# RoPE on one core: the last software load cut into 16 and 48 rows instead of 32 and 32, and GpSimd's first store tied to the 16

## The chip, the cores and the metric

The kernel runs on one core of one Trainium2 chip. The metric is device microseconds (us) of that core for one execution. Before the change the median of 11 runs is 85.08 us, from 84.03 to 87.63. The profile that is read below is of one execution that took 85.83 us, of which 84.1 us are the profiled span.

## The reference

```python
def setup_inputs():
    batch, n_heads, seq, head_dim = 8, 8, 1024, 64
...
    angles = np.outer(positions, freqs)
    cos = np.cos(angles)
    sin = np.sin(angles)
    x_first, x_second = x[:, :, :, :half], x[:, :, :, half:]
    out_first = x_first * cos - x_second * sin
    out_second = x_first * sin + x_second * cos
    return np.concatenate([out_first, out_second], axis=-1).astype(np.float32)
```

`x` has 8 x 8 = 64 heads of 1024 rows of 64 float32 values. One head is 256 KB, all of `x` is 16.8 MB, and so is the output. `positions` has 1024 whole numbers and `freqs` 32 floats.

## The kernel before, in words

**Tiling.** A head is cut into 16 chunks of 64 rows (`C = 64`), and one chunk lies in one partition, as a run of 64 x 64 = 4096 values (`run`). Eight heads fill 128 partitions (`G = 8`). `groups` (line 43) lists eight groups: the first has six heads (96 partitions), the other seven have eight heads. The two heads left over (`edge = 2`, heads 0 and 1) take another way: SP loads them in float32 (line 69) and stores them at the very end (line 175).

**Loads.** GpSimd issues all loads of the groups at the start (lines 77 to 83). They convert float32 in HBM to bf16 in SBUF on the way, so that a partition's run is 16 KB when it is read and 8 KB when it lands. Each group is one DMA, apart from the last group, which comes as two: the first 32 rows of every chunk and then the other 32. That makes nine DMAs. The DMA semaphores are used in turn, eight of them, so the ninth load waits until the first has landed (10.37 us).

**Tables.** VectorE (DVE) and ScalarE (ACT) make the sine and cosine tables of the chunked layout (`tables`, line 92). A second, smaller pair of tables, for the two edge heads, is made after the third group (lines 153 to 156). The instruction that rounds the turns is line 99.

**Rotation.** For each group DVE does three operations (`rotate`, line 134): a product with the sine (line 138), a product with the cosine (139) and a sum with the two halves swapped (141).

**Stores.** GpSimd issues one store for each group (line 151), which converts bf16 to float32 on the way out. All loads and all stores of the groups go through GpSimd's one software DMA queue, q0. Ahead of the first store stands line 145, an instruction that does nothing but wait until the first part of the last group's load has landed:

```python
    nc.gpsimd.keepalive_nop(ins=[nc.gpsimd.lower_ap(xts[-1][:, :run // 2])])
```

Behind it, each store waits in order for the sum of its group. By then several groups are ready.

**End.** SP waits for the landing of all group stores but the last (lines 172 and 173), issues two stores of 256 KB for the edge heads (line 175), and waits for the end of everything (lines 176 to 178).

Of the kernel before, what the change touches and what calls it, by code (L numbers as in the profile page):

```python
# [10 lines left out]
def kernel(  # L11
# [7 lines left out]
    nc = tc.nc  # L19
# [6 lines left out]
    b, h, seq, d = x.shape  # L26
# [14 lines left out]
    run = C * d  # L41
    first = G - edge
    groups = [(edge, first)] + [(g, G) for g in range(G, bh, G)]
# [7 lines left out]
    def hbm(t, lo, n, a=0, b=run):  # L51
        return bass.AP(tensor=t.tensor, offset=t.offset + lo * head + a,
                       ap=[[run, n * chunks], [1, b - a]])
# [14 lines left out]
    for i in range(edge):  # L68
        nc.sync.dma_start(out=xf[:, i], in_=hbm_head(x, i))
    nc.scalar.dma_start(  # L70
        out=pos_i[:chunks].bitcast(positions.dtype),
        in_=bass.AP(tensor=positions.tensor, offset=positions.offset, ap=[[C, chunks], [1, C]]))
    nc.scalar.dma_start(out=fr[0:P:32], in_=freqs[None, :].to_broadcast([P // 32, half]))


    xts = []
    for lo, n in groups:
        xt = xpool.tile([P, run], bf16, name="xt")[:n * chunks]
        parts = 2 if lo == groups[-1][0] else 1
        for a in range(0, run, run // parts):  # L80
            b = a + run // parts
            nc.gpsimd.dma_start(out=xt[:, a:b], in_=hbm(x, lo, n, a, b))  # L82
        xts.append(xt)
    half_pi = singles.tile([P, 1], f32)
    nc.gpsimd.memset(half_pi, math.pi / 2)
# [28 lines left out]
    for q in range(0, P, 32):  # L114
        v.tensor_copy(out=pos_f[q:q + 32],  # L115
                      in_=pos_i.rearrange("p (c w) -> p c w", w=words)[:, :, :1])
# [5 lines left out]
        out=pos_r.bitcast(positions.dtype),  # L122
        in_=bass.AP(tensor=positions.tensor, offset=positions.offset,
                    ap=[[R, P], [1, R], [1, 1]])))
# [17 lines left out]
        return ot  # L142


    nc.gpsimd.keepalive_nop(ins=[nc.gpsimd.lower_ap(xts[-1][:, :run // 2])])

    stored = []
    for i, ((lo, n), xt) in enumerate(zip(groups, xts)):
# [60 lines left out]
```

## Time and profile before

| what | us |
|---|---|
| median of 11 runs | 85.08 (84.03 to 87.63) |
| the profiled execution | 85.83 |
| its span | 84.1 |
| DVE busy | 65.1 |
| ACT busy | 9.4 |
| POOL (GpSimd) busy | 10.1 |
| ninth load issued | 10.37 |
| first store issued | 42.35 |
| last group store issued | 71.39 |
| SP's two stores issued | 77.12 |

The span is the time from the first to the last recorded instruction of the execution; what lies around it is 85.83 - 84.1 = 1.73 us. The page cuts the span into 40 slices of 2.1 us; a digit is the busy share of a slice in tenths. Its GB/s count the bytes on the destination's side, so that a load that lands as bf16 shows half of what it reads. HBM read is 16.79 MB and written 16.78 MB, 399 GB/s over the span.

### The profile page before, as it was taken

To read this page: it belongs to the slowest core of one execution; us is meant where nothing else is said; L and a number is where in the kernel's file an instruction comes from. 1 tells how busy PE (TensorE), PEld (TensorE's weight loads), DVE (VectorE), ACT (ScalarE), POOL (GpSimd) and SP (SyncE) were. 2 spreads that over 40 slices of the span, in tenths; PEclk is the share of its full clock that TensorE was granted. 3 is DMA by queue.
4 is the path that set the end of the run, shared out by engine and by line. 5 is a ranking of instruction groups with operands and counts; after the bars stand their busy time and mean duration, and the time that the engine had idled before them with its cause. 6 is when DMAs were issued, how large, how long until landed. Compare 5 with 4: busy or idle time off the path is not lost.

```text
span 84.1 us, 155 instructions
## 1 busy us (share of the span) xinstructions
DVE 65.1 (77%) x46; ACT 9.4 (11%) x8; POOL 10.1 (12%) x22
## 2 busy tenths in 40 slices
DVE  0125995499999999999999999999999999900000
ACT  0600004997000000000006000000000000000000
POOL 4960050000000000000081000200200200200000
DMA  2999999999999999999969999999999999999992
GB/s 16 296 211 187 203 210 222 210 226 207 220 208 218 214 214 218 210 211 209 185 222 413 413 452 398 468 405 452 421 444 429 437 429 405 460 413 444 405 389 110
DMA packets 3144, 25.45 MB, mean 303 GB/s; under 512 B 504, under 2 KB 520, under 8 KB 1288
## 3 DMA queue, kind: packets, MB, share of 16 engines
q0 software_dynamic: 2384, 24.38, 94.9%
q1 hardware_dynamic: 576, 1.05, 3.7%
q10 hardware_dynamic: 184, 0.02, 0.3%
HBM read 16.79 MB, written 16.78 MB: 399 GB/s over the span
## 4 chain that ended last, share of the span: by engine, by line
DVE 65%; issue 12%; DMA 7%; ACT 2%; ACTq 1%
DVE ot L139 21%; DVE ot L141 16%; DVE t L138 14%; DMA const<-in_freqs_dram 7%; DVE turnsc L95 3%; DVE turnsc L101 3%; ACT sinc L105 2%; DVE wholec L99 1%; DVE last L166 1%; DVE last L163 1%; DVE sinc L106 1%; DVE t L163 1%; ACTq L70 1%; DVE turnsr L95 0%; DVE turnsr L101 0%
## 5 line engine op out<-in xcount | busy, mean ns | idle before, releaser
L138 DVE TENSOR_TENSOR t<-xt,sinc 128x4096 bf16<-128x4096 bf16 (+1 forms) x8 | 18.2, 2281 | 0.0
L139 DVE TENSOR_TENSOR ot<-xt,cosc 128x4096 bf16<-128x4096 bf16 (+1 forms) x8 | 18.2, 2281 | 0.0
L141 DVE TENSOR_TENSOR ot<-ot,t 128x4096 bf16<-128x4096 bf16 (+1 forms) x8 | 18.2, 2280 | 0.0
L151 POOL DMA_DIRECT2D out_dram<-ot x8 | 4.2, 533 | 56.0 <-DMA xt<-in_x_dram 30.7
L82 POOL DMA_DIRECT2D xt<-in_x_dram x9 | 5.6, 640 | 5.6 <-DMA xt<-in_x_dram 4.7
L105 ACT ACTIVATE sinr<-turnsr 128x256 bf16<-128x256 f32 x1 | 0.4, 417 | 23.4 <-DVE turnsr L101 23.4
L105 ACT ACTIVATE sinc<-turnsc 128x2048 bf16<-128x2048 f32 x1 | 1.9, 1909 | 9.9 <-DVE turnsc L101 9.9
L101 DVE TENSOR_TENSOR turnsc<-turnsc,wholec 128x2048 f32<-128x2048 f32 x1 | 2.3, 2293 | 0.0
L95 DVE TENSOR_TENSOR turnsc<-pos_f,fturn 128x2048 f32<-128x2048 f32 x1 | 2.3, 2293 | 0.0
L106 DVE TENSOR_SCALAR sinc<-sinc 128x2048 bf16<-128x2048 bf16 x1 | 0.7, 694 | 2.0 <-ACT sinc L105 2.0
L87 DVE LOAD_MASK_SELECT const<-const x1 | 0.0, 14 | 2.8 <-DMA const<-in_positions_dram 2.8
L109 ACT ACTIVATE cosc<-wholec,half_pi 128x2048 bf16<-128x2048 f32 x1 | 2.0, 2002 | 0.1
L108 ACT ACTIVATE wholec<-turnsc 128x2048 f32<-128x2048 f32 x1 | 1.9, 1894 | 0.0
L88 DVE LOAD_MASK_SELECT const<-const x1 | 0.0, 14 | 2.4 <-DMA const<-in_freqs_dram 2.4
L105 ACT ACT_TABLE_LOAD x1 | 1.3, 1283 | 2.6 <-issue 2.6
L99 DVE TENSOR_SCALAR wholec<-turnsc 128x2048 f32<-128x2048 f32 x1 | 1.2, 1226 | 0.0
L166 DVE TENSOR_TENSOR last<-last,t 128x1024 f32<-128x1024 f32 x1 | 1.2, 1225 | 0.0
L163 DVE TENSOR_TENSOR last<-x,cosr 128x1024 f32<-128x1024 bf16 x1 | 1.2, 1214 | 0.0
L126 ACT CAST x<-xf 128x1024 bf16<-128x1024 f32 x1 | 1.0, 1028 | 0.0
L115 DVE CAST pos_f<-const 32x64 f32<-32x64 int32 x4 | 0.8, 194 | 0.1
L64 DVE MEMSET const<- 128x160 int32 x1 | 0.2, 192 | 0.8 <-PEq L193 0.8
L109 ACT ACTIVATE cosr<-wholer,half_pi 128x512 bf16<-128x512 f32 x1 | 0.7, 722 | 0.0
(15 smaller groups left out, 3.7 us busy)
## 6 DMA issues: line engine op xcount, KB each, us to landing
out_dram<-ot POOLq DMA_DIRECT2D x7, 2048.0 KB, 12.4
xt<-in_x_dram POOLq DMA_DIRECT2D x6, 1024.0 KB, 23.8
out_dram<-ot POOLq DMA_DIRECT2D x1, 1536.0 KB, 5.5
xt<-in_x_dram POOLq DMA_DIRECT2D x2, 512.0 KB, 35.2
xt<-in_x_dram POOLq DMA_DIRECT2D x1, 768.0 KB, 8.8
xf<-in_x_dram SPq DMA_DIRECT2D x2, 256.0 KB, 2.9
out_dram<-last SPq DMA_DIRECT2D x2, 256.0 KB, 5.5
const<-in_positions_dram ACTq DMA_DIRECT2D x1, 8.0 KB, 2.7
```

What stands on the lines that cost most here:

```text
L82: nc.gpsimd.dma_start(out=xt[:, a:b], in_=hbm(x, lo, n, a, b))
L95: v.tensor_mul(out=turns, in0=pos_f.to_broadcast([P, n, half]), in1=fturn.to_broadcast([P, n, half]))
L99: v.tensor_scalar(out=whole, in0=turns, scalar1=magic, scalar2=magic, op0=Alu.add, op1=Alu.subtract)
L101: v.tensor_sub(out=turns, in0=turns, in1=whole)
L105: nc.scalar.activation(out=sin[:, :, 0], in_=turns, func=Act.Sin, scale=twopi)
L109: nc.scalar.activation(out=cos, in_=whole[:, :, None, :].to_broadcast([P, n, copies, half]), func=Act.Sin, scale=-twopi, bias=half_pi)
L138: v.tensor_mul(out=t.rearrange(flat), in0=xt, in1=sin_c[:n].rearrange(flat))
L139: v.tensor_mul(out=ot, in0=xt.rearrange("p (c two h) -> p c two h", two=2, h=half), in1=cos_c[:n].to_broadcast([n, C, 2, half]))
L141: v.tensor_add(out=ot, in0=ot, in1=swap(t))
L151: nc.gpsimd.dma_start(out=hbm(out, lo, n), in_=ot.rearrange("p c two h -> p (c two h)")))
L163: v.tensor_mul(out=o, in0=x0, in1=w.rearrange("p r two h -> p (r two h)")[:, None, :].to_broadcast(flat))
L166: v.tensor_add(out=last.rearrange(rows, two=2, h=half), in0=last.rearrange(rows, two=2, h=half), in1=swap(t.rearrange(rows, two=2, h=half)))
```

## The change

The last group's two loads are cut at 16 rows instead of 32. The first part has 1024 values a partition (4 KB read, 2 KB landed), the second 3072 (12 KB read, 6 KB landed). The number of DMAs and their order are as before. Line 145 waits for the first part, which is now the 16 rows.

```diff
+    first_part = run // 4
     xts = []
     for lo, n in groups:
         xt = xpool.tile([P, run], bf16, name="xt")[:n * chunks]
-        parts = 2 if lo == groups[-1][0] else 1
-        for a in range(0, run, run // parts):
-            b = a + run // parts
-            nc.gpsimd.dma_start(out=xt[:, a:b], in_=hbm(x, lo, n, a, b))
+        cut = first_part if lo == groups[-1][0] else run
+        for a, b in ((0, cut), (cut, run)):
+            if a < b:
+                nc.gpsimd.dma_start(out=xt[:, a:b], in_=hbm(x, lo, n, a, b))
         xts.append(xt)
...
-    nc.gpsimd.keepalive_nop(ins=[nc.gpsimd.lower_ap(xts[-1][:, :run // 2])])
+    nc.gpsimd.keepalive_nop(ins=[nc.gpsimd.lower_ap(xts[-1][:, :first_part])])
```

## The prediction

> **What bounds the kernel now.** I read the page's slices first.
>
> ```profile
> DVE  0125995499999999999999999999999999900000
> DMA  2999999999999999999969999999999999999992
> ```
>
> DVE ends five slices before the end; DMA is at 9 in every slice from the second to the last but one, with one dip, slice 21 (42.0 to 44.1 us). So the kernel is a string of transfers: all loads, then all stores. The chain of waits follows DVE, which is no contradiction: it doesn't see that a store stands in the DMA queue behind others. The trace's semaphore events confirm the string. A full group load lands every 4.87 us (last engine at 14.84, 19.71, 24.60, 29.48, 34.34, 39.21), a full store likewise (47.88, 52.75, ... 81.92). Both move 2 MB on the HBM side: 2.097 MB / 4.87 us = 431 GB/s.
>
> Next the dip, in the stretches view (columns: us, busy time of DVE, ACT and POOL, clock, DMA share, GB/s):
>
> ```profile
> 40.00:41.00 1.00, 1.00 (x1) 0.00 (x0) 0.00 (x0) 1.00 1.05 213
> 41.00:42.00 1.00, 1.00 (x3) 0.00 (x0) 0.00 (x0) 1.00 0.83 164
> 42.00:43.00 1.00, 1.00 (x1) 0.00 (x0) 0.65 (x2) 1.00 0.19 37
> 43.00:44.00 1.00, 1.00 (x3) 0.04 (x1) 1.00 (x3) 1.00 0.73 283
> ```
>
> Against the 1.05 of full work the three stretches lose 0.22 + 0.86 + 0.32 = 1.40 us, as a mean over 16 DMA engines. The waits and the timeline name the wait in front of the first store:
>
> ```profile
> POOL out_dram L151 <- DMA xt<-in_x_dram: 30.7, 1, 30.7
> ```
> ```profile
> 41.11 0.28 DVE L99 TENSOR_SCALAR wholer<-turnsr 128x256 f32<-128x256 f32 x1
> 41.31 2.28 DVE L141 TENSOR_TENSOR ot<-ot,t 128x4096 bf16<-128x4096 bf16 x1
> 42.35 2.11 POOL L151 DMA_DIRECT2D out_dram<-ot  x4 [30.67 <-DMA xt<-in_x_dram]
> ```
>
> The share 0.19 is the clue: 0.19 x 16 = 3 engines work on while 13 stand idle. The trace's single DMA packets and landings say the same. Each DMA raises its semaphore 16 times, once an engine. The first 32 rows landed on 13 engines at 39.48 to 39.95, on the other three at 41.23, 41.53, 41.67. Three engines are 1.7 us behind; they were so from the first load (7.73 to 8.00 against 9.59 to 10.09), where packets of 1.5 to 2.0 us stand in place of 0.63. The 13 ended their loads at 41.6 to 42.1, the three at 43.46, 43.64, 43.77. The first store packets start at 43.44 on the idle engines, and at 43.6 to 43.8 on the last ones. **So the three late engines never waited**: their store packets were queued (43.44) before their own loads ended. The dip belongs to the 13 that are ahead.
>
> **What the Trainium skill says.** "DMA: Bandwidth & Descriptors", section "Why a DMA increments its semaphore by 16 and not by 1": with a software DMA all 16 engines post their +1, and only the full count says that it has landed. So the slowest engine opens line 145, as the landings here show. Same page, "Where 436 GB/s comes from": 16 ports of 32 B at 850 MHz, 435 GB/s; the 431 measured is at that, in loads and stores. A lane at its own ceiling can't be helped by others: while 13 engines were idle, the three late ones' packets took 322 to 324 ns, as when all worked. "SBUF — State Buffer", section "SBUF: two separate sides": a DVE operation in a two-port mode keeps GpSimd from writing its DMA descriptors, until its end + about 115 ns. The trace agrees: the ninth load's issue took 1.20 us instead of the 0.54 to 0.65 of the others, beside line 99's float32 operation (10.22 to 11.45), and ended at 11.57.
>
> **The change part by part.** I work in the profiled span.
>
> 1. *First part.* Half a load took 41.67 - 39.21 = 2.46 us for 8 packets an engine: 307 ns each for 4 KB landed; 8 KB takes 4.87 / 8 = 609. The slope is 302 ns for 4 KB, the fixed part 5 ns. A 2 KB packet is then 5 + 151 = 156 ns (estimate), eight are 1.25 us, and the slowest engine lands at 39.21 + 1.25 = 40.46, 1.21 us earlier.
> 2. *Second part.* A 6 KB packet is 5 + 453 = 458 ns (estimate), eight are 3.66. Both parts: 4.91 us against 4.92 before. No packet is added (8 + 8 an engine), no DMA either. So the loads end when they ended: 41.6 to 42.1, and 43.77 on the last engine. The nearest rows don't show a 6 KB packet; from packet lengths instead (324 and 625 ns) the fixed part is 2 x 324 - 625 = 23 ns. At one extra packet a row that is 8 x 23 = 0.18 us; from below it can't gain, the bytes being the same. I take 0.
> 3. *The issues.* The ninth load is issued at 10.37 as before, since it waits for the first load, not for its size; its 1.20 us hide behind 30 us of queued loads. No load is queued later.
> 4. *The wait at line 145.* From landing to issue it took 42.35 - 41.67 = 0.68, from issue to the first store packet 43.44 - 42.35 = 1.09. Now: issue at 41.14, packets at 42.23. Line 99's small operation (41.11 to 41.39) may hold the issue until 41.39 + 0.12 and a further 0.5 at most: packets at 42.23 to 42.6. It covers itself: nobody but the 13 idle engines waits.
> 5. *Behind it on GpSimd*: the stores of groups 1 to 4. Groups 1 to 3 have been ready since 38.65, so they are issued at 41.1, 41.7, 42.2. Group 4's sum ends at 43.59, so its issue moves only from 43.93 to about 43.7. Three stores are 22 heads, 5.8 MB, at 431 GB/s some 13 us of work, so no engine runs dry; later stores are issued at 53.2, 59.8, 66.4, 71.4 by DVE, at least 5.6 us ahead of the landing of the store before (the seventh lands at 77.05).
> 6. *The 13 engines* start stores at about 42.3 instead of 43.5: 1.2 us ahead. **The three late ones start at 43.5 to 43.8, as before.** From there each has 62 store packets of 608 ns: 43.77 + 37.7 = 81.5; the last group's packets ended at 81.54. Nothing moves.
> 7. *SP* issues its two stores after the seventh store's last landing (77.05, issue at 77.12), which a late engine sets. Their packets follow the last group's on each engine (81.1 to 82.8). Unmoved.
>
> Sum on the path: 0 + 0 + 0, less at most 0.1 us where an engine now ahead had been last at the end. Span 84.1 to 84.0; that execution took 85.83, and would take 85.8. Against the median of the runs, 85.08 - 0.05, I say 85.0.
>
> If in another execution no engine is late, the first half lands at about 39.95, store packets are there at 39.95 + 1.77 = 41.72, and the loads end at 41.6 to 42.1. There is no dip to close either, or one of 0.1 us.
>
> **Rivals.**
>
> *A, the dip is the gain.* If the work left were shared among all engines, the signal's 1.21 us would come off: 85.08 - 1.21 = 83.9. For it: the dip is real, 1.40 us. Against it: every store puts 8 packets on each engine (the first one 6), whichever is free, and the three late engines stay 1.7 us behind through all seven loads without catching up. Chance 0.08.
>
> *B, reads and writes collide (slower).* 13 engines would write for 1.5 us while three read. Where stores began at 44.1, single packets took 951, 904 and 780 ns instead of 642, up to 48% more. Were the late engines' last 1.5 us stretched so, it is +0.7; doubled, and lasting, +1.5: 85.8 to 86.6. It passes 1% from a stretch of 57% (0.85 / 1.5). Against it: the late engines' last load packets, between 43.44 and 43.77, ran beside writes and took 324 ns at most. Chance 0.09.
>
> *C, the 6 KB rows are cut small (slower).* At 23 ns a packet and 8 rows an engine, 1% (0.85 us) takes 5 more packets a row; 512 B pieces (12 a row) cost 8 x 11 x 23 ns = 2.0: 87.1. Rows of 8 KB and 16 KB stay whole in the trace. Chance 0.05.
>
> **How the numbers follow.** My case (nothing moves, within 0.3 us either way) has 0.78. About 1% is what a measurement of this kernel can tell from no change. Faster by over 1%: A, 0.08, and 0.01 from the tail of my case. Slower: B and C, 0.14. Within 1%: 0.77. The range goes down to A (84.0) and up to the whole of B (86.6), leaving out C; the likeliest case alone is 84.7 to 85.3.
>
> **What would show it.** Right: the first part lands on the last engine near 40.5 and the first store is issued near 41.1; the dip in the slices is gone or small; first store landings spread over about 1.5 us (the engines ahead near 46.4, the late ones near 47.8) instead of 0.41; SP's stores at about 77.1. Wrong: SP's issue a full us earlier (A); load packets over 324 ns after 42.3 (B); more than 16 load packets of the last group an engine (C); or an execution in which even the last engine had stood idle before.

## The result, and the profile after

The changed kernel takes 85.67 us (median of 12 runs, 84.80 to 87.02), the kernel before, run beside it, 85.53 us (47 runs, 83.80 to 87.63). The ratio is 1.0098, 95% interval 1.0057 to 1.0139: slower by about 0.8 us. The two medians hide most of that, because in many executions of these kernels a few DMA engines fall 1 to 2 us behind at the start, and the ratio leaves out the executions with the longest times. The shortest spans agree with it: 82.0 to 82.1 us many times in the timed executions of the kernel before, 82.7 in the shortest of the changed kernel's twelve.

The profiled execution of the changed kernel took 84.81 us, with a span of 82.7. That is less than the 84.1 of the profile before, though the kernel is slower: no engine fell behind in it (first load landed at 7.52 to 7.91 on all 16), whereas three had in the other. Two single profiles of this kernel can't be compared by their spans.

The slices of the changed kernel (same rows as before, with GB/s added):

```profile
DVE  0147993699999999999999999999999999930000
DMA  1999999999999999999999999999999999999992
GB/s 16 309 222 218 206 226 202 226 218 202 228 208 214 226 202 230 206 193 167 223 399 412 452 412 444 444 412 444 412 444 444 412 452 404 444 444 412 460 344 76
```

The dip in DMA is gone, but this profile doesn't show that the change closed it: no engine is late here, and for such an execution the prediction expected no dip, or one of 0.1 us, in the kernel before either. The GB/s row has a dip where the DMA row shows none: it falls to 193 and 167 in slices 18 and 19 (35 to 39 us), from some 214. The engines are busy there, but they move less. The wait and the first stores:

```profile
POOL out_dram L152 <- DMA xt<-in_x_dram: 30.9, 1, 30.9
```
```profile
39.73 1.59 POOL L152 DMA_DIRECT2D out_dram<-ot  x3 [30.89 <-DMA xt<-in_x_dram]
40.54 0.36 DVE L100 TENSOR_SCALAR wholer<-turnsr 128x256 f32<-128x256 f32 x1
43.38 0.53 POOL L152 DMA_DIRECT2D out_dram<-ot  x1 [2.07 <-DVE ot L142]
```

The first three stores go out together and the fourth waits for DVE, as forecast. The stretches of the changed kernel (us, DVE, ACT, POOL, clock, DMA share, GB/s):

```profile
36.00:37.00 1.00, 1.00 (x1) 0.00 (x0) 0.00 (x0) 1.00 0.84 162
37.00:38.00 1.00, 1.00 (x2) 0.00 (x0) 0.00 (x0) 1.00 1.07 143
38.00:39.00 1.00, 1.00 (x3) 0.00 (x0) 0.00 (x0) 1.00 1.18 209
39.00:40.00 1.00, 1.00 (x1) 0.00 (x0) 0.27 (x1) 1.00 1.04 215
40.00:41.00 1.00, 1.00 (x3) 0.00 (x0) 1.00 (x3) 1.00 0.98 203
41.00:42.00 1.00, 1.00 (x1) 0.00 (x0) 0.31 (x1) 1.00 1.09 266
42.00:43.00 1.00, 1.00 (x1) 0.00 (x0) 0.00 (x0) 1.00 1.05 416
43.00:44.00 1.00, 1.00 (x3) 0.54 (x2) 0.53 (x1) 1.00 1.16 475
```

and of the kernel before where its 32-row part begins:

```profile
36.00:37.00 1.00, 1.00 (x2) 0.00 (x0) 0.00 (x0) 1.00 0.80 164
37.00:38.00 1.00, 1.00 (x1) 0.00 (x0) 0.00 (x0) 1.00 1.11 225
38.00:39.00 1.00, 1.00 (x3) 0.00 (x0) 0.00 (x0) 1.00 1.05 213
```

From 37 to 38 us the engines are as busy as ever (1.07 against 1.11) and move 143 instead of 225 GB/s. (The 36-to-37 line is alike in both: a packet counts where it starts.) The single packets of the trace say why. There are 128 packets of 2 KB for the 16 rows. The 48 that start before 37.03 us take 172 or 173 ns each; of the 80 that start later, 56 take longer, up to 414 ns, and the mean of the 80 is 258. The 6 KB packets take 474, apart from seven that start between 38.13 and 38.78 us and take 484 to 600.

**A measure that leaves out what happens at the start.** I count from the landing of the seventh group's load on its last engine to the last landing of SP's stores. So the 1 to 2 us that an engine lost in the first load drop out. The parts are differences of the trace's landing events, each on its last engine, in us:

| profiled execution | 7th load lands | first part | whole 8th load | from 7th load to the end |
|---|---|---|---|---|
| before | 39.21 | 2.46 | 4.93 | 43.96 |
| before, again | 39.02 | 2.46 | 4.93 | 44.01 |
| before, third | 39.76 | 2.46 | 5.00 | 43.95 |
| changed kernel | 37.16 | 1.89 | 5.70 | 44.63 |

The eighth load takes 5.70 - 4.93 = 0.77 us longer, and 1.89 - 1.25 = 0.64 of it lies in the first part, measured against the forecast. The end comes 44.63 - 43.96 = 0.67 us later, counted from the same point. The ratio says 0.8 us, with an interval of about 0.5 to 1.2, so 0.67 agrees with it.

### The profile page after: what moved, and what is told of

It reads as the page before. It is cut to its first block, busy times and chain, and to the rows that moved or that the text cites. A ratio compares the mean times of both kernels' runs of the same rounds, so it can differ in the third digit from the quotient of the medians.

```text
span 82.7 us, 155 instructions
## 1 busy us (share of the span) xinstructions
DVE 65.5 (79%) x46; ACT 9.4 (11%) x8; POOL 9.5 (11%) x22
## 4 chain that ended last, share of the span: by engine, by line
DVE 66%; issue 12%; DMA 6%; ACT 2%; ACTq 1%
DVE ot L140 21%; DVE ot L142 16%; DVE t L139 14%; DMA const<-in_freqs_dram 6%; DVE turnsc L102 3%; DVE turnsc L96 3%; ACT sinc L106 2%; DVE wholec L100 1%; DVE last L167 1%; DVE last L164 1%; DVE sinc L107 1%; DVE t L164 1%; ACTq L70 1%; DVE turnsr L96 0%; DVE turnsr L102 0%
## 5 line engine op out<-in xcount | busy, mean ns | idle before, releaser
L83 POOL DMA_DIRECT2D xt<-in_x_dram x9 | 4.9, 566 | 3.4 <-DMA xt<-in_x_dram 2.6
```

## The experiments

Two theories run through the expectations. The first says that the 16 rows cost, being short rows that leave gaps in HBM. It is called S at first and R later; G and L are two forms of it. The rival, called C at first and W later, says that the early store costs, because stores are queued behind loads that still run.

**The early wait on the loads of before.** Stores as early as can be, no short rows:

```diff
-    nc.gpsimd.keepalive_nop(ins=[nc.gpsimd.lower_ap(xts[-1][:, :run // 2])])
+    nc.gpsimd.keepalive_nop(ins=[nc.gpsimd.lower_ap(xts[-2])])
```

> Loads as in the kernel before (32 and 32 rows), but the first store waits for the seventh group's load, not for a part of the eighth, so it is queued some 2 us before the loads end. Theory S (rows of 4 KB load slowly; the early store is harmless): no short rows, so no loss; ratio to before 0.995 to 1.003, both parts of the last load take 2.45 us each. Theory C (stores queued behind loads that still run collide with them): the stores come even earlier than in the changed kernel, ratio 1.01 or more, and load packets of the last part longer than 330 ns.

Measured: ratio 1.0101 (1.0059 to 1.0143), 85.86 us over 22 runs. This spoke for C. But in its profile, which has one late engine, no load packet was stretched: whole eighth load 4.92, from seventh load to end 43.88, the same as before. The wait opened only when the late engine had landed, so this store was not very early:

```profile
39.76 1.72 POOL L151 DMA_DIRECT2D out_dram<-ot  x3 [28.12 <-DMA xt<-in_x_dram]
```

The loads of the other fifteen engines landed at 41.74 to 42.28, some 2 us later.

**The same wait with 16 and 48 rows, without a cut, and with four parts.** In the changed kernel the same wait; in the kernel before `parts = 1`, or `parts = 4 if lo == groups[-1][0] else 1`, each with that wait.

> Loads as in the changed kernel (16 and 48 rows), the first store waits for the seventh group's load. Theory S: the 16 rows take about 1.9 us again instead of 1.25, ratio to before 1.006 to 1.012. Theory C: ratio 1.01 or more as well, but then the half-and-half kernel with the same wait is as slow; the pair tells it apart.

Measured: ratio 1.0124 (1.0030 to 1.0219), 6 runs. First part 2.41, whole load 6.14, to the end 45.08. The first store went out at 38.42, before the first part had landed (40.16), so both causes can be in these numbers.

> The eighth load in one DMA (no cut), the first store waits for the seventh group's load. Theory S: no short rows; the last load takes 4.87 us, ratio to before 0.990 to 1.002. Theory C: ratio 1.01 or more.

Measured: ratio 1.0075 (1.0040 to 1.0110), 22 runs. A miss for S: whole load 6.03, to the end 45.03, with 8 KB packets stretched from 39.0 us on (44 of them, up to 1311 ns instead of 625) and no short row anywhere. Its first store went out at 37.87.

> The eighth load in four DMAs of 16 rows each, the first store waits for the seventh group's load. Theory S: the loss of 0.64 us comes up to four times, the eighth load takes 6.5 to 7.5 us instead of 4.87, ratio to before 1.02 to 1.03. Theory C: as the half-and-half kernel with the same wait, 1.01.

Measured: ratio 1.0173 (1.0094 to 1.0253), 4 runs, a little less than theory S said. Its profile shows much less than S said: the four parts took 1.54, 1.32, 1.22 and 1.23, whole load 5.31 instead of 6.5 to 7.5, to the end 44.31. Only the first of four equal parts was much stretched. So in this execution short rows at a step of 16 KB were not slow for good, but for the first 1 to 2 us after the rows had become short.

So far both theories had something in their favour.

**The short rows with the store held back.** In the changed kernel, behind the wait:

```diff
+    pause = singles.tile([P, 1536], f32)
+    tc.keep_in_program_order(nc.gpsimd.memset(pause, 0.0))
```

> The changed kernel (16 and 48 rows) with a memset of about 1.2 us on GpSimd between the wait and the first store, so that the store is queued about when the kernel before queues it. Theory R (the 16 rows themselves load slowly, whenever the store comes): the ratio stays that of the changed kernel, 1.006 to 1.014, and the first part takes well over 1.25 us. Theory W (the early store is what costs, as the half-and-half kernel with the early wait was slower without any short rows): ratio back to 0.997 to 1.004.

Measured: ratio 1.0082 (1.0021 to 1.0143), 6 runs. The memset took 1.49 us and the first store went out at 42.67, against 42.16 to 42.90 in the three profiles of the kernel before:

```profile
41.23 1.49 POOL L148 MEMSET pause<- 128x1536 f32 x1 [29.55 <-DMA xt<-in_x_dram]
```
```profile
37.00:38.00 1.00, 1.00 (x1) 0.00 (x0) 0.00 (x0) 1.00 1.03 186
38.00:39.00 1.00, 1.00 (x3) 0.00 (x0) 0.00 (x0) 1.00 1.12 180
39.00:40.00 1.00, 1.00 (x1) 0.00 (x0) 0.00 (x0) 1.00 1.02 184
40.00:41.00 1.00, 1.00 (x1) 0.00 (x0) 0.00 (x0) 1.00 0.99 195
```

Three us at full share and 180 to 186 GB/s, before any store was issued. First part 2.08, whole load 5.82, to the end 44.75: 0.8 over before. So the short rows cost by themselves, without an early store, and they do in an execution with late engines too.

**Profiles of the kernel before, and of the early wait, again.** Nothing changed in either.

> The kernel before once more, for a profile of an execution in which no DMA engine falls behind at the start. Both theories: span about 82.0, the first half lands on the last engine within 2.5 us of the seventh load, no packet of the last load longer than 330 ns, first store packets about when the loads end. If long packets show near the end of the loads here too, neither theory tells the kernels apart by them.

> The half-and-half kernel with the early wait once more, for a profile of an execution without engines that fall behind. Theory W: packets of the last loads, or the first stores, are stretched by some 0.7 us an engine, span 82.6 to 82.9. Theory R: none is, span 82.0 to 82.2, and its slower time has another place.

Measured: both executions had late engines. The kernel before gave 44.01 from seventh load to end, the early wait 43.89, with a span of 83.9 each. This early-wait execution is the test of the dip, because it has three late engines, as the profile in the prediction has. Its DMA share held between 1.02 and 1.15 from 40 to 44 us:

```profile
40.00:41.00 1.00, 1.00 (x1) 0.00 (x0) 1.00 (x3) 1.00 1.08 217
41.00:42.00 1.00, 1.00 (x3) 0.00 (x0) 0.36 (x1) 1.00 1.15 315
42.00:43.00 1.00, 1.00 (x1) 0.00 (x0) 0.00 (x0) 1.00 1.02 365
43.00:44.00 1.00, 1.00 (x3) 0.00 (x0) 0.03 (x1) 1.00 1.06 410
```

There is no dip, and 0.06 to 0.12 us are gained, about what the prediction had allowed.

> The kernel before, for a profile in which no DMA engine falls behind at the start, to set beside the changed kernel's. If the early wait costs something of its own there: span 81.9 to 82.2, no long packet between 36 and 44 us. If not: span 82.6 or more, as the changed kernel.

> The half-and-half kernel with the early wait, for a profile without engines that fall behind. If the early wait costs something of its own there: packets between 39 and 43 us stretched by 0.6 us an engine or more, span 82.6 or more, beside a kernel before at 82.0. If not: span as the kernel before.

Measured: the kernel before had late engines again (43.95), so a profile of it without any is missing. The four timed runs of it, an identical kernel, gave the ratio 1.0222 (1.0110 to 1.0334) to itself: a ratio from four to six runs is not to be trusted here to 1%, and the three above that rest on so few are read by their stages. So is the early wait's 1.0149 (0.9951 to 1.0346) from four runs here. Its profile had no late engine, and there the early wait does cost: second half 3.55 instead of 2.47, to the end 44.93:

```profile
37.79 1.05 POOL L151 DMA_DIRECT2D out_dram<-ot  x2 [29.07 <-DMA xt<-in_x_dram]
```
```profile
39.00:40.00 1.00, 1.00 (x2) 0.00 (x0) 0.54 (x1) 1.00 1.17 217
40.00:41.00 1.00, 1.00 (x1) 0.00 (x0) 0.00 (x0) 1.00 0.89 127
41.00:42.00 1.00, 1.00 (x3) 0.00 (x0) 0.00 (x0) 1.00 1.18 246
```

Its first store went out at 37.79, 5.3 us ahead of the end of its loads at 43.1; in the changed kernel it is 39.73, with loads that end at 42.9.

**The changed kernel without gaps.** The same two DMAs in bytes, packets and waits, at other HBM addresses:

```diff
-                nc.gpsimd.dma_start(out=xt[:, a:b], in_=hbm(x, lo, n, a, b))
+                nc.gpsimd.dma_start(out=xt[:, a:b], in_=hbm(x, lo, n, a, b) if cut == run else bass.AP(
+                    tensor=x.tensor, offset=x.offset + lo * head + a * P, ap=[[b - a, P], [1, b - a]]))
```

> The changed kernel, but both parts of the last load read HBM without gaps: 128 rows of 4 KB one after the other, then 128 of 12 KB. The same bytes, DMAs, packets and waits; the last group's rows land permuted, so its output rows stand in other places than the reference's. Theory G (the 16 rows are slow because 4 KB are read at a step of 16 KB): no stretched packets, first part 1.25 us, the slowest executions as in the kernel before, ratio to before below 1.006 or what the early wait alone costs (1.010). Theory L (4 KB rows are slow at the change from 16 KB rows, wherever they lie): packets of 200 to 400 ns again, first part 1.9 us, ratio as the changed kernel or more.

Measured: ratio 1.0006 (0.9971 to 1.0041), 22 runs, fastest 83.92. First part 1.29, whole load 4.95, to the end 43.92, no load packet of it stretched:

```profile
37.00:38.00 1.00, 1.00 (x1) 0.00 (x0) 0.00 (x0) 1.00 1.06 203
38.00:39.00 1.00, 1.00 (x2) 0.00 (x0) 0.00 (x0) 1.00 1.21 242
39.00:40.00 1.00, 1.00 (x2) 0.00 (x0) 0.00 (x0) 1.00 1.06 217
```

This settles it. The early signal is the changed kernel's own, the HBM addresses alone are other, and the loss is gone. The profile has four late engines, as the one with the store held back (first part 2.08), so late engines are not the difference.

**The same small first part, cut by heads.** 32 partitions with whole 16 KB rows, then 96:

```diff
-        parts = 2 if lo == groups[-1][0] else 1
-        for a in range(0, run, run // parts):
-            b = a + run // parts
-            nc.gpsimd.dma_start(out=xt[:, a:b], in_=hbm(x, lo, n, a, b))
+        cut = 2 if lo == groups[-1][0] else n
+        for a, b in ((0, cut), (cut, n)):
+            if a < b:
+                nc.gpsimd.dma_start(out=xt[a * chunks:b * chunks], in_=hbm(x, lo + a, b - a))
...
-    nc.gpsimd.keepalive_nop(ins=[nc.gpsimd.lower_ap(xts[-1][:, :run // 2])])
+    nc.gpsimd.keepalive_nop(ins=[nc.gpsimd.lower_ap(xts[-1][:2 * chunks])])
```

> The last load is cut by heads: two heads (32 partitions, whole rows of 16 KB, 512 KB without gaps) and then six heads (96 partitions). The first store waits for the two heads, as many bytes as the changed kernel's 16 rows. Theory G (4 KB at a step of 16 KB is what is slow): no stretched packets, first part about 1.25 us, ratio to before 0.995 to 1.004. If the early signal or the small first part costs by itself: 1.006 or more.

Measured: ratio 0.9984 (0.9955 to 1.0013), 22 runs, fastest 83.95. First part 1.44, whole load 4.96, to the end 43.90:

```profile
37.00:38.00 1.00, 1.00 (x1) 0.00 (x0) 0.00 (x0) 1.00 1.07 221
38.00:39.00 1.00, 1.00 (x1) 0.00 (x0) 0.00 (x0) 1.00 1.06 221
39.00:40.00 1.00, 1.00 (x3) 0.00 (x0) 0.06 (x1) 1.00 0.94 197
```

It gives the early signal without the cost: the store is issued at 39.94, and no slice of DMA has a dip. It isn't measurably faster than the kernel before. As a test of the dip this profile is weak, since its one late engine is only 1 us behind; that the dip is worth 0.1 us or so is shown by the early wait's profiles with late engines.

**The early wait, held back by 2 us.** The half-and-half kernel with the early wait and a memset of 128 x 2048 behind it:

> The half-and-half kernel that waits for the seventh group's load, with a memset of about 2 us on GpSimd ahead of the first store, so that it is issued near 39.8 us where no engine falls behind, as in the changed kernel, instead of 37.8. If what made the half-and-half kernel slower is that stores are issued 4 us ahead of the end of the loads: ratio back to 0.997 to 1.004, second half in 2.5 us. If any store queued behind running loads costs: ratio 1.006 to 1.012 as without the pause.

Measured: ratio 0.9999 (0.9968 to 1.0031), 22 runs. The memset took 1.80 us and the first store went out at 39.99. Its profile, with one engine a little late, has a whole load of 5.46 and 44.39 to the end. Its second half took 3.01 us, where 2.5 was expected, with three packets stretched to at most 642 ns. So some stretching is left, but over 22 runs no cost is to be seen. The runs differ from the early wait by the pause alone, so what made the early wait slow was how early its stores went out: near 37.8 us where no engine is late, 2 us earlier than in the changed kernel.

## Why the prediction was wrong

**The step that failed is the first one, "First part".** It priced the 16 rows at 8 x 156 ns = 1.25 us, on a line through the packets of 4 KB and 8 KB as they land (8 KB and 16 KB as they are read). They took 1.89 us in the changed kernel and 2.08 with the store held back. With the early wait they took 2.41, where stores may have added to it, and 1.54 as the first of four equal parts. The same number of bytes in packets of the same size took 1.29 us without gaps in HBM. So the packet price was right to 0.04 us, and the term that was missing is the address pattern: 4 KB read at each step of 16 KB. I had looked for an unknown in the 6 KB rows of step 2 and bounded those; the 2 KB packets, as little shown in the trace, got no bound from above. Rows of 8 KB at the same step (the 32 rows of before, 2.46 us in all three executions) lose nothing, so a straight line through them couldn't show that rows of 4 KB do.

**Step 2** (6 KB packets of 458 ns, uncut): right in kind. There were 128 of them, eight an engine. Without gaps in HBM the part took the 3.66 us of the forecast; in the changed kernel it took 3.81, with seven of its first packets stretched.

**Steps 3 to 5** (issues, the wait, what is queued behind): right. From landing to issue 39.73 - 39.05 = 0.68, the figure used. Three stores went out at once, the fourth behind its sum at 43.38. DVE's small operation ran at 40.54, beside the second store's issue, and held nothing up: that issue took 0.54.

**Steps 6 and 7** (the late engines set the end, so closing the dip gains 0 to 0.1): the changed kernel's own profile has no late engine and tests neither. The early wait's two profiles with late engines do, and there both steps were right. From the seventh load they ended 0.06 to 0.13 us sooner than the kernel before. In the second of them the first store landed from 45.56 to 47.70 us, a spread of 2.1 us where before had 0.41: the engines ahead had started early, and the late ones set the end.

**So the sum was 0 + 0 + 0 - 0.1 and should have been 0.64 + 0.15 + 0 - 0.1 = 0.7**, against 0.67 in the profile from the seventh load to the end and about 0.8 by the ratio. The measured 85.67 us lies in the range of 84.0 to 86.6, and a ratio of 1.0098 is just within the 1% that was given 0.77. That was luck: the prediction had time "within 1%" because nothing was to move, and the interval, 1.0057 to 1.0139, tells the loss from nothing.

**The rivals.** A, the dip as the gain, fell: in the early wait with late engines the dip went, and 0.1 us went with it, not 1.21. B, reads beside writes, fell as the cause: the loss stands in packets that started between 37.0 and 38.8 us, ahead of the first store's issue at 39.73, and is there with the store held back. C, 6 KB rows cut small, fell: none was cut. The kernel was slower in a way that no rival had.

**Open.** Why rows of 4 KB at a step of 16 KB are slow, and why only at first in the one run that shows it (1.54 us, then 1.32, 1.22, 1.23 in four equal parts), no run shows. Nor does any show why very early stores stretch the last loads' packets. What the profiles do show is when: in the two executions of half and whole loads where the store went out some 5.3 us ahead of the end of the loads (37.79 and 37.87; 44.93 and 45.03 to the end), and not in the two where the wait opened with a late engine and it went out at 39.76 and 39.77, some 2 us before the loads of the other engines landed (43.88, 43.89). Where between them the cost begins isn't measured.

## What to carry to other kernels

A transfer cut into parts can have a price that its bytes and packets don't show: the addresses that the parts read. Here the cut at 32 rows cost nothing and the cut at 16 rows 0.64 us in its first part, while a cut along whole rows (by heads), of the same number of bytes, cost nothing that the ratio shows. So price a cut by a measurement of that very pattern, and look at GB/s beside the busy share, since a stretched packet counts as a busy engine (1.07 at 143 GB/s). And ask of an idle stretch which engines idle: here those that ended last were not among them, and filling it gained 0.1 us.

## What the runs showed of the hardware

In eight of the fourteen profiled executions, of this kernel and its relatives, one or more DMA engines were 1 to 2 us behind from the very first load (it landed on the last engine at 9.68 to 10.54 us, against 7.80 to 8.10 in four others), and they kept most of that distance through all the loads: in the first profile of the kernel before, first and last engine landed 2.4 us apart in the first load and 2.2 in the last. In no profile did the other engines make it up for them. So the changed kernel's profile can have a span 1.4 us shorter than that of the kernel before, though the changed kernel is the slower one.
